# Reordering the preparation of a seven-product step in the FFN's down projection, and the last output scaling

## The chip, the cores and the metric

The kernel runs on one core of a Trainium2 chip. The metric is device time in microseconds; the kernel before took 1753.55 us (median of 3 runs, 1753.36 to 1753.64). The engines are named as the profile names them: PE (TensorE matmul), PEld (its weight loads), DVE (VectorE), ACT (ScalarE), POOL (GpSimd), SP (the queue that issues most DMAs).

## What is computed

One decoder layer on 256 tokens of width 2048, in float32: a normalisation, one combined projection, dilated-window attention beside a gated recurrence, an output projection with a residual, and a feed-forward part. The change lies in the last of these lines, the down projection (5632 to 2048 columns) and the norm and residual behind it:

```python
a = rmsnorm(h, norm_ffn_pre[layer])
gt, up = jnp.split(a @ w_ffn_gate_up[layer], [D_FF], axis=-1)
ff = (jax.nn.silu(gt) * up) @ w_ffn_down[layer]
h = h + rmsnorm(ff, norm_ffn_post[layer])
```

## The kernel before

**Precision.** Every float32 operand is split in two parts: a high part (fp32r, made by a copy on ACT) and a low part (the operand minus its high part, made by a subtraction on DVE). A product of two operands is three matmuls: high x high, high x low, low x high.

**Steps of the down projection.** The output has 2048 columns, taken in two blocks of 1024 (two groups of 512). Each block runs over 22 steps; a step takes 256 rows of the weights (a tile `raw` of 128 x 2048) and the matching two chunks of the activation (`act`, 2 x 128 x 256). The 256 tokens are two sides of 128.

- An **ordinary step** makes 2 sides x 2 groups x 2 chunks = 8 products, so 24 matmuls.
- A **seven-product step** makes the same 2 x 2 x 2 block product from 7 products of sums and differences of sub-blocks (a Strassen-Winograd scheme), so 21 matmuls, and pays for it with sums of the weights and sums of the activation. There are six of them in each block, every third step (`DOWN`): steps 4, 7, ..., 19 of the first block and 3, 6, ..., 18 of the second. The first of its products uses `dh` and `dl`, the high and low parts of three of the four raw weight sub-blocks; `dl` is the last tile that is prepared.

**Preparation of a step** (`split_wide`) first calls `prep_act`, which splits the activation (`a`: high on ACT L410, low on DVE L411). For a seven-product step it also makes four sums `s` of the activation on DVE (L379, L379, L382, L383, in `seven_sums`), their high part `so` on ACT (L384) and low part on DVE (L385). After that it treats the weights. For an ordinary step this is the high part `w` (ACT L305) and the low part `wl` (DVE L306). For a seven-product step it is three DVE instructions for the sums `sum` (L310, L316, L317), their high parts `w` on ACT (L315, L318), `dh` on ACT (L320), and the low parts `wl` (L321) and `dl` (L322) on DVE.

**What sets the order.** The schedule is manual: each engine runs its instructions in the order in which the program writes them, and waits for another engine or a DMA at the head of its queue. The main loop writes, for each step i: the preparation of step i+2, the load of step i+5 (SP, L289, two DMAs of 512 KB), the matmuls of step i, and evacuation work of an earlier block. The buffers bound how far an engine can run ahead: 3 of `raw`, 3 of `w`, 3 of `wl`, 1 each of `sum`, `dh`, `dl`. So the high part of step i+2 needs the `w` buffer that PE frees when it has finished step i-1, and the load of step i+5 needs the `raw` buffer that ACT and DVE free when they have prepared step i+2.

**The end.** The last three steps are run side by side, and `finish(i, j)` handles side i and column group j = 2, 3. It adds the partial result (L1191, `down_sum`), squares it on ACT with a running sum (L1195, `down_square`), and for j = 2 multiplies by the gain (`down_gain`, L1200). For j = 3 it computes the norm factor `r3` (`rsqrt_mean`: DVE L127, L129, L133 and ACT L125, L126), then writes four stores, each a DVE instruction (L1241: result times `r3` plus residual) and a DMA. The gain multiplication of group 3 stands ahead of the last store.

Of the kernel before, what the change touches and what calls it, by code (L numbers as in the profile page):

```python
# [13 lines left out]
F32 = mybir.dt.float32  # L14
F32R = mybir.dt.float32r
I32 = mybir.dt.int32
AF = mybir.ActivationFunctionType
# [60 lines left out]
def tile_hybrid_block(ctx: ExitStack, tc: tile.TileContext, t, out):  # L78
    nc = tc.nc
# [12 lines left out]
    def nm(s):  # L92
        serial[0] += 1
        return f"{s}_{serial[0]}"

    def rslot(s):
        return rpool.tile([P, 1024], F32R, tag="r", bufs=16, name=nm(s))
# [10 lines left out]
    def p3(s, dtype, n, bufs, tag=None):  # L108
        return act_pool[0].tile([P, n], dtype, tag=tag or s, bufs=bufs, name=nm(s))
# [7 lines left out]
    def rsqrt_mean(dst, ss, n, bias=None):  # L117

        w = ss.shape[-1]
        v, y, a = (small(s)[:, :w] for s in ("v", "y", "a"))
        bias = bias or (eps[:, 0:1], eps[:, 1:2])
        nc.scalar.activation(y, ss, AF.Ln, scale=1.0 / n, bias=bias[0])  # L125
        nc.scalar.activation(y, y, AF.Exp, scale=-0.5)  # L126
        nc.vector.tensor_scalar(v, ss, -0.5 / n, bias[1], op0=OP.mult, op1=OP.add)  # L127
        if w == 1:
            nc.vector.scalar_tensor_tensor(out=a, in0=y, scalar=v, in1=y, op0=OP.mult, op1=OP.mult)  # L129
        else:  # L130
            nc.vector.tensor_mul(a, y, y)
            nc.vector.tensor_mul(a, a, v)
        nc.vector.scalar_tensor_tensor(  # L133
            out=dst, in0=a, scalar=1.5, in1=y, op0=OP.add, op1=OP.mult
        )
# [31 lines left out]
    def ptile(s):  # L167
        pool, n = (act_pool[0], 2) if act_pool else (fp, 5)
        return pool.tile([P, 512], F32, tag="p", bufs=n, name=nm(s))
# [58 lines left out]
    def wslot():  # L228
        return stream.tile([P, 2048], F32R, tag="w", bufs=N_SPLIT, name=nm("w"))
# [65 lines left out]
    def split_wide(n):  # L295

        if n >= len(steps):
            return
        b, i, raw = steps[n][:3]
        m, by7 = b.order[i]  # L300
        if b.prep:
            b.prep(m, by7)
        hi, lo = wslot(), p3("wl", F32R, 2048, 3)
        if not by7:
            nc.scalar.activation(hi, raw, AF.Copy)  # L305
            nc.vector.tensor_sub(lo, raw, hi.bitcast(F32))  # L306
            steps[n][3] = hi, lo
            return
        s, d = p3("sum", F32, 2048, 1), raw[:, 512:]
        nc.vector.tensor_sub(  # L310
            s[:, :1024].rearrange("p (a c) -> p a c", a=2),
            raw[:, 512:1536].rearrange("p (a c) -> p a c", a=2),
            raw[:, None, :512].to_broadcast([P, 2, 512]),
        )
        nc.scalar.activation(hi[:, :1024], s[:, :1024], AF.Copy)  # L315
        nc.vector.tensor_add(s[:, 1024:1536], raw[:, 512:1024], s[:, 512:1024])  # L316
        nc.vector.tensor_sub(s[:, 1536:], raw[:, 1536:], s[:, 1024:1536])  # L317
        nc.scalar.activation(hi[:, 1024:], s[:, 1024:], AF.Copy)  # L318
        dhi, dlo = p3("dh", F32R, 1536, 1), p3("dl", F32R, 1536, 1)
        nc.scalar.activation(dhi, d, AF.Copy)  # L320
        nc.vector.tensor_sub(lo, s, hi.bitcast(F32))  # L321
        nc.vector.tensor_sub(dlo, d, dhi.bitcast(F32))  # L322
        steps[n][3] = hi, lo, dhi, dlo

# [49 lines left out]
    def seven_sums(f, dst):  # L374

        s = ptile("s").rearrange("p (n t) -> p n t", n=4)
        a11, a12, a21, a22 = f[:, 0, :P], f[:, 1, :P], f[:, 0, P:], f[:, 1, P:]
        for o, x, c, y in ((0, a21, -1.0, a22), (1, s[:, 0, :], -1.0, a11)):
            nc.vector.scalar_tensor_tensor(  # L379
                out=s[:, o, :], in0=x, scalar=c, in1=y, op0=OP.mult, op1=OP.subtract  # L380
            )
        nc.vector.tensor_sub(s[:, 2, :], a11, a21)  # L382
        nc.vector.tensor_sub(s[:, 3, :], a12, s[:, 1, :])  # L383
        nc.scalar.activation(dst[:, 0], s, AF.Copy)  # L384
        nc.vector.tensor_sub(dst[:, 1], s, dst[:, 0].bitcast(F32))  # L385

    def sums_of(dst):
        return lambda n: (dst[:, 0, n, :], dst[:, 1, n, :])


    class Split:
# [14 lines left out]

        def put(self, n, src):

            x = self.slots[n]
            nc.scalar.activation(x[:, :, 0, :], src, AF.Copy)  # L410
            nc.vector.tensor_sub(x[:, :, 1, :], src, x[:, :, 0, :].bitcast(F32))  # L411
            self.there.add(n)

# [677 lines left out]
    def h_sums():  # L1091

        for m in H7:
            f = ptile("f").rearrange("p (k t) -> p k t", k=2)
            x = hT[0].slots[m]
            nc.vector.tensor_add(f, x[:, :, 0, :].bitcast(F32), x[:, :, 1, :].bitcast(F32))
            dst = p3("so", F32R, 1024, 4).rearrange("p (z n t) -> p z n t", z=2, n=4)
            yield
            seven_sums(f, dst)
            h7[m] = sums_of(dst)  # L1100
            yield

# [71 lines left out]
            )  # L1174

    def prep_act(m, by7):
        f = act_t[m // 2][:, m % 2 * 2 : m % 2 * 2 + 2, :]
        x = parts_of[m] = Split("a", 2)
        x.put(0, f)
        if by7:  # L1180
            dst = rslot("so").rearrange("p (z n t) -> p z n t", z=2, n=4)
            seven_sums(f, dst)
            a7[m] = sums_of(dst)

    def act(k):
        return parts_of[k // 2](k % 2)

    def down_sum(j, i, b):

        f = b.rest[i, j % 2]  # L1190
        nc.vector.tensor_add(f, b.bank[i, j % 2], f)  # L1191

    def down_square(j, i, b):
        sq, r2 = fss[0][:, 4 * i + j : 4 * i + j + 1], r2c[:, i : i + 1]
        nc.scalar.activation(ptile("junk"), b.rest[i, j % 2], AF.Square, scale=r2, accum_out=sq)  # L1195

    def down_gain(j, i, b):
        if i == 0:
            fz[j] = p3("fz", F32, 1024, 4, "so").rearrange("p (b c) -> p b c", b=2)
        nc.vector.scalar_tensor_tensor(  # L1200
            out=fz[j][:, i, :], in0=b.rest[i, j % 2], scalar=r2c[:, i : i + 1],
            in1=fpost[j // 2][:, (j % 2) * 512 : (j % 2 + 1) * 512],
            op0=OP.mult, op1=OP.mult,
        )
# [11 lines left out]
    def so_far_of(ss, i):  # L1216

        b = small("base")
        nc.vector.tensor_reduce(
            b[:, 0:1], ss[:, 4 * i : 4 * i + 3], op=OP.add, axis=mybir.AxisListType.X  # L1220
        )
        nc.vector.tensor_scalar(b[:, 0:1], b[:, 0:1], 1.0 / D, EPS, op0=OP.mult, op1=OP.add)
        nc.vector.tensor_scalar(b[:, 1:2], b[:, 0:1], -0.5, None, op0=OP.mult)
        return b[:, 0:1], b[:, 1:2]
# [3 lines left out]
    def finish(i, j):  # L1228

        b = wides[-1]  # L1230
        down_sum(j, i, b)
        down_square(j, i, b)
        if j == 2:
            down_gain(j, i, b)
            bases[i] = so_far_of(fss[0], i)
            return
        sq, r3 = fss[0][:, 4 * i + 3 : 4 * i + 4], r3c[:, i : i + 1]

        def store(j, lo=0, hi=512, eng=nc.sync):
            z = fz[j][:, i, lo:hi]  # L1240
            nc.vector.scalar_tensor_tensor(  # L1241
                out=z, in0=z, scalar=r3, in1=h_t[j][:, i, lo:hi], op0=OP.mult, op1=OP.add
            )
            eng.dma_start(out[0, i * P : (i + 1) * P, j * 512 + lo : j * 512 + hi], z)

        rsqrt_mean(r3, sq, D, bases[i])
        store(0, 0, 128)
        store(0, 128, 512, nc.scalar)
        store(1)
        store(2, eng=nc.scalar)  # L1250
        down_gain(3, i, b)
        store(3)


# [52 lines left out]
    for j in range(2):  # L1307
        add_wide_block(t["w_ffn_down"][0], (1024 * j, 1024 * j + 512), DOWN[j], act,
                       lambda m: a7[m], evac_down, prep=prep_act,
                       pre=begin_down if j == 0 else None, turn=3 if j == 0 else None)  # L1310
# [14 lines left out]
    for i in range(len(chunks)):  # L1325
        b, c = chunks[i][:2]
# [17 lines left out]
    for i in range(len(steps)):  # L1344
        b, c = steps[i][:2]
# [22 lines left out]
    for g in range(2):  # L1368
        multiply_wide(last, (0,), (g,))
        finish(0, 2 + g)  # L1370
    for g in range(2):
        for i in (last - 2, last - 1, last):
            multiply_wide(i, (1,), (g,))
        finish(1, 2 + g)
# [51 lines left out]
```

## Time and profile before

| | |
|---|---|
| median of the runs | 1753.55 us |
| the profiled execution's own time | 1753.68 us |
| its span | 1751.9 us |
| DVE busy over the span | 1265.1 us (72%) |
| ACT busy over the span | 885.0 us (51%) |
| first matmul of the down projection | starts at 1500.83 us |
| last matmul of the program | starts at 1741.25 us |
| last DVE instruction | starts at 1747.80 us, lasts 0.75 us |

How to read it: times are from the start of the span. The down projection is the last seventh of it, and only this stage is touched by the change. Matmuls are pipelined: a row of PE lasts 0.39 us while the next starts 0.23 us later, so PE's busy share says little, and stalls of PE are read from the distance between starts. DVE's rows overlap a little too: a 128x2048 subtraction lasts 2.28 us and the next instruction starts 2.20 us after it.

### The profile page before, as it was taken

How to read it: one execution, taken by the hardware profiler on the slowest of the kernel's cores; microseconds unless marked ns; L12 is line 12 of the kernel's file. 1: busy time of each engine (PE TensorE's matmuls, PEld its weight loads, DVE VectorE, ACT ScalarE, POOL GpSimd, SP SyncE). 2: the span in 40 equal slices, each digit the busy share in tenths (PEclk: the TensorE clock that was granted, in tenths of full speed). 3: DMA queues.
4: the chain of work that ended last, by engine and by line, in shares of the span. 5: the costliest groups of instructions: out<-in, count | busy, mean ns of one | idle time of the engine just before them, and what ended most of it. 6: DMA issues, size and time to landing. Idle time of an engine off the chain costs nothing.

```text
span 1751.9 us, 21592 instructions
## 1 busy us (share of the span) xinstructions
PE 1730.3 (99%) x8424; PEld 1449.0 (83%) x8424; DVE 1265.1 (72%) x1372; ACT 885.0 (51%) x1050; POOL 74.1 (4%) x54
## 2 busy tenths in 40 slices
PE   9999999999999999999999999999999999999997
PEld 7888888888888888888888877888888888878775
DVE  5657657877546775544565577888888888888887
ACT  6545445344444444454444465555555555565563
POOL 0002404300000000000000000000000000000000
PEclk9999999999999999999999999999999999999999
DMA  7655444455455554455555745555555555656553
GB/s 265 204 191 193 144 162 151 145 165 182 159 169 169 189 188 161 159 175 193 194 183 189 268 157 203 194 192 193 204 206 204 201 194 192 223 181 218 183 183 117
DMA packets 201223, 325.92 MB, mean 186 GB/s; under 512 B 10096, under 2 KB 76832, under 8 KB 201120
## 3 DMA queue, kind: packets, MB, share of 16 engines
q1 hardware_dynamic: 198848, 319.41, 54.2%
q10 hardware_dynamic: 2272, 5.12, 0.8%
q8 instruction: 66, 1.08, 0.2%
q14 instruction: 37, 0.30, 0.1%
HBM read 322.40 MB, written 2.10 MB: 185 GB/s over the span
## 4 chain that ended last, share of the span: by engine, by line
PE 82%; DVE 12%; ACT 3%; issue 2%; DMA 1%; POOL 0%; SPq 0%; DVEq 0%; ACTq 0%
PE acc L115 65%; PE aux L115 16%; DVE wl L306 3%; DVE wl L321 1%; DVE dl L322 1%; DVE a L411 1%; DVE sum L310 1%; ACT w L318 1%; DVE w L243 1%; DVE sum L317 0%; DVE sum L316 0%; ACT w L242 0%; DVE w L667 0%; ACT so L384 0%; DVE s L379 0%
## 5 line engine op out<-in xcount | busy, mean ns | idle before, releaser
L243 DVE TENSOR_TENSOR w<-raw,w 128x1024 fp32r<-128x1024 f32 (+1 forms) x353 | 444.2, 1260 | 366.4 <-ACT w L242 364.3
L242 ACT ACTIVATE w<-raw 128x1024 fp32r<-128x1024 f32 (+1 forms) x353 | 373.0, 1057 | 483.1 <-PE acc L115 472.1
L115 PE MATMUL acc<-w,xT 128*128 128x512 f32 x1728 | 407.9, 394 | 0.0
L115 PEld LDWEIGHTS acc<-w,xT 128*128 128x128 f32 x1728 | 325.1, 190 | 65.7 <-DVE w L243 0.3
L115 PE MATMUL acc<-xT,w 128*128 128x512 f32 (+1 forms) x2048 | 365.5, 340 | 0.0
L115 PEld LDWEIGHTS acc<-xT,w 128*128 128x128 f32 x2048 | 314.8, 189 | 46.1
L306 DVE TENSOR_TENSOR wl<-raw,w 128x2048 fp32r<-128x2048 f32 x82 | 187.4, 2285 | 19.9 <-ACT w L305 19.9
L305 ACT ACTIVATE w<-raw 128x2048 fp32r<-128x2048 f32 x82 | 156.4, 1908 | 59.0 <-PE aux L115 27.0
L115 PE MATMUL acc<-w,hT 128*128 128x512 f32 x622 | 182.5, 392 | 1.5 <-DVE w L243 1.2
L115 PEld LDWEIGHTS acc<-w,hT 128*128 128x128 f32 x622 | 115.8, 188 | 27.0 <-DVE w L243 2.5
L115 PE MATMUL aux<-w,hT 128*128 128x512 f32 x430 | 135.6, 389 | 0.0
L321 DVE TENSOR_TENSOR wl<-sum,w 128x2048 fp32r<-128x2048 f32 x42 | 96.3, 2292 | 47.3 <-ACT w L318 47.3
L115 PEld LDWEIGHTS aux<-w,hT 128*128 128x128 f32 x430 | 80.7, 188 | 16.8
L315 ACT ACTIVATE w<-sum 128x1024 fp32r<-128x1024 f32 x42 | 44.6, 1063 | 96.3 <-DVE sum L310 92.0
L115 PE MATMUL acc<-w,yT 128*128 128x512 f32 x384 | 88.0, 390 | 0.2 <-DVE w L243 0.2
L115 PEld LDWEIGHTS acc<-w,yT 128*128 128x128 f32 x384 | 71.9, 188 | 15.4 <-DVE w L243 0.6
L115 PE MATMUL acc<-w,a 128*128 128x512 f32 x268 | 83.7, 389 | 0.0
L115 PE MATMUL aux<-w,a 128*128 128x512 f32 x268 | 83.7, 389 | 0.0
L115 PE MATMUL aux<-wl,hT 128*128 128x512 f32 x215 | 83.6, 389 | 0.0
L115 PE MATMUL acc<-wl,hT 128*128 128x512 f32 x215 | 83.6, 389 | 0.0
L322 DVE TENSOR_TENSOR dl<-raw,dh 128x1536 fp32r<-128x1536 f32 x42 | 73.5, 1751 | 0.0
L320 ACT ACTIVATE dh<-raw 128x1536 fp32r<-128x1536 f32 x42 | 61.9, 1473 | 0.0
(263 smaller groups left out, 2016.9 us busy)
## 6 DMA issues: line engine op xcount, KB each, us to landing
raw<-in_w_in SPq DMA_DIRECT2D x271, 512.0 KB, 4.5
raw<-in_w_ffn_gate_up SPq DMA_DIRECT2D x176, 512.0 KB, 4.4
raw<-in_w_ffn_down SPq DMA_DIRECT2D x88, 512.0 KB, 4.9
raw<-in_w_mix_out SPq DMA_DIRECT2D x32, 512.0 KB, 4.9
raw<-in_w_attn_branch SPq DMA_DIRECT2D x16, 512.0 KB, 4.6
raw<-in_w_hgrn_branch SPq DMA_DIRECT2D x16, 512.0 KB, 4.6
hx<-in_x ACTq DMA_DIRECT2D x4, 512.0 KB, 9.9
x<-in_x SPq DMA_DIRECT2D x3, 512.0 KB, 10.4
```

The lines of the kernel that those rows point to most:

```text
L115: nc.tensor.matmul(ps, lhsT, rhs, start=start, stop=stop, skip_group_check=True)
L242: nc.scalar.activation(wh[:, k], raw[:, k], AF.Copy)
L243: nc.vector.tensor_sub(wl[:, k], raw[:, k], wh[:, k].bitcast(F32))
L305: nc.scalar.activation(hi, raw, AF.Copy)
L306: nc.vector.tensor_sub(lo, raw, hi.bitcast(F32))
L310: nc.vector.tensor_sub(s[:, :1024].rearrange("p (a c) -> p a c", a=2), raw[:, 512:1536].rearrange("p (a c) -> p a c", a=2), raw[:, None, : ...
L315: nc.scalar.activation(hi[:, :1024], s[:, :1024], AF.Copy)
L318: nc.scalar.activation(hi[:, 1024:], s[:, 1024:], AF.Copy)
L320: nc.scalar.activation(dhi, d, AF.Copy)
L321: nc.vector.tensor_sub(lo, s, hi.bitcast(F32))
L322: nc.vector.tensor_sub(dlo, d, dhi.bitcast(F32))
L411: nc.vector.tensor_sub(x[:, :, 1, :], src, x[:, :, 0, :].bitcast(F32))
```

## The change

The generator `prep_act` is cut into pieces, and `split_wide` calls the pieces at chosen places. An ordinary step keeps its order. In a seven-product step the activation's high part still comes first; then the sums of the weights and their high parts; then the activation's low part and its four sums with their high part; then `dh` and `wl`; then the low part `so` of the activation's sums; and `dl` last. In the gate-up blocks no activation is prepared, so nothing moves there. In `finish`, the gain multiplication of group 3 moves up, to directly behind the square that ACT computes.

```diff
         b, i, raw = steps[n][:3]
         m, by7 = b.order[i]
-        if b.prep:
-            b.prep(m, by7)
+        prep = b.prep(m, by7) if b.prep else iter(())
+        next(prep, None)
         hi, lo = wslot(), p3("wl", F32R, 2048, 3)
         if not by7:
             nc.scalar.activation(hi, raw, AF.Copy)
+            next(prep, None)
             nc.vector.tensor_sub(lo, raw, hi.bitcast(F32))
...
         nc.scalar.activation(hi[:, 1024:], s[:, 1024:], AF.Copy)
+        next(prep, None)
         dhi, dlo = p3("dh", F32R, 1536, 1), p3("dl", F32R, 1536, 1)
         nc.scalar.activation(dhi, d, AF.Copy)
         nc.vector.tensor_sub(lo, s, hi.bitcast(F32))
+        next(prep, None)
         nc.vector.tensor_sub(dlo, d, dhi.bitcast(F32))
...
         nc.scalar.activation(dst[:, 0], s, AF.Copy)
-        nc.vector.tensor_sub(dst[:, 1], s, dst[:, 0].bitcast(F32))
+        return lambda: nc.vector.tensor_sub(dst[:, 1], s, dst[:, 0].bitcast(F32))
...
-            seven_sums(f, dst)
+            seven_sums(f, dst)()
...
         x = parts_of[m] = Split("a", 2)
-        x.put(0, f)
+        x.high(0, f)
+        yield
+        x.low(0, f)
         if by7:
             dst = rslot("so").rearrange("p (z n t) -> p z n t", z=2, n=4)
-            seven_sums(f, dst)
+            low = seven_sums(f, dst)
             a7[m] = sums_of(dst)
+            yield
+            low()
...
         down_square(j, i, b)
+        down_gain(j, i, b)
         if j == 2:
-            down_gain(j, i, b)
             bases[i] = so_far_of(fss[0], i)
             return
...
         store(2, eng=nc.scalar)
-        down_gain(3, i, b)
         store(3)
```

**DVE, the first seven-product step of the down projection.** The names are those of the section on the kernel; `act` is the activation, `a` its parts. Before:

```order
L411 TENSOR_TENSOR a_11413<-act_8972,a_11413 128x2x256
L379 SCALAR_TENSOR_TENSOR s_11417<-act_8972 128x128
L379 SCALAR_TENSOR_TENSOR s_11417<-s_11417,act_8972 128x128
L382 TENSOR_TENSOR s_11417<-act_8972 128x128
L383 TENSOR_TENSOR s_11417<-act_8972,s_11417 128x128
L385 TENSOR_TENSOR so_11416<-s_11417,so_11416 128x512
L310 TENSOR_TENSOR sum_11426<-raw_11300 128x1024
L316 TENSOR_TENSOR sum_11426<-raw_11300,sum_11426 128x512
L317 TENSOR_TENSOR sum_11426<-raw_11300,sum_11426 128x512
L321 TENSOR_TENSOR wl_11425<-sum_11426,w_11424 128x2048
L322 TENSOR_TENSOR dl_11433<-raw_11300,dh_11432 128x1536
```

The same step on DVE in the changed kernel:

```order
L311 TENSOR_TENSOR sum_11417<-raw_11300 128x1024
L317 TENSOR_TENSOR sum_11417<-raw_11300,sum_11417 128x512
L318 TENSOR_TENSOR sum_11417<-raw_11300,sum_11417 128x512
L420 TENSOR_TENSOR a_11413<-act_8972,a_11413 128x2x256
L382 SCALAR_TENSOR_TENSOR s_11425<-act_8972 128x128
L382 SCALAR_TENSOR_TENSOR s_11425<-s_11425,act_8972 128x128
L385 TENSOR_TENSOR s_11425<-act_8972 128x128
L386 TENSOR_TENSOR s_11425<-act_8972,s_11425 128x128
L323 TENSOR_TENSOR wl_11416<-sum_11417,w_11415 128x2048
L388 TENSOR_TENSOR so_11424<-s_11425,so_11424 128x512
L325 TENSOR_TENSOR dl_11432<-raw_11300,dh_11431 128x1536
```

The three sums of the weights moved to the front, and the low part `so` moved from behind the activation's sums to between `wl` and `dl`.

**ACT, the same step.** Before:

```order
L410 ACTIVATE a_11413<-act_8972 128x2x256
L384 ACTIVATE so_11416<-s_11417 128x512
L315 ACTIVATE w_11424<-sum_11426 128x1024
L318 ACTIVATE w_11424<-sum_11426 128x1024
L320 ACTIVATE dh_11432<-raw_11300 128x1536
```

And in the changed kernel:

```order
L416 ACTIVATE a_11413<-act_8972 128x2x256
L316 ACTIVATE w_11415<-sum_11417 128x1024
L319 ACTIVATE w_11415<-sum_11417 128x1024
L387 ACTIVATE so_11424<-s_11425 128x512
L322 ACTIVATE dh_11431<-raw_11300 128x1536
```

On ACT only the high part `so` moved, from ahead of the two high parts of the weights' sums to behind them.

**DVE, the end of the program (side 1, group 3).** Here `e` is the partial result, `fss` the sums of squares from ACT, `fz` the output tiles, `h` the residual. Before:

```order
L1191 TENSOR_TENSOR e_12954<-acc_12238,e_12954 128x512
L127 TENSOR_SCALAR v_13084<-fss_11334,base_13059 128x1
L129 SCALAR_TENSOR_TENSOR a_13086<-y_13085,v_13084 128x1
L133 SCALAR_TENSOR_TENSOR r3c<-a_13086,y_13085 128x1
L1241 SCALAR_TENSOR_TENSOR fz_12247<-fz_12247,r3c,h_7825 128x128
L1241 SCALAR_TENSOR_TENSOR fz_12247<-fz_12247,r3c,h_7825 128x384
L1241 SCALAR_TENSOR_TENSOR fz_12302<-fz_12302,r3c,h_7860 128x512
L1241 SCALAR_TENSOR_TENSOR fz_13002<-fz_13002,r3c,h_7903 128x512
L1200 SCALAR_TENSOR_TENSOR fz_13033<-e_12954,r2c,fpost_11337 128x512
L1241 SCALAR_TENSOR_TENSOR fz_13033<-fz_13033,r3c,h_7967 128x512
```

In the changed kernel:

```order
L1205 TENSOR_TENSOR e_12954<-acc_12238,e_12954 128x512
L1214 SCALAR_TENSOR_TENSOR fz_13017<-e_12954,r2c,fpost_11337 128x512
L127 TENSOR_SCALAR v_13085<-fss_11334,base_13059 128x1
L129 SCALAR_TENSOR_TENSOR a_13087<-y_13086,v_13085 128x1
L133 SCALAR_TENSOR_TENSOR r3c<-a_13087,y_13086 128x1
L1255 SCALAR_TENSOR_TENSOR fz_12247<-fz_12247,r3c,h_7825 128x128
L1255 SCALAR_TENSOR_TENSOR fz_12247<-fz_12247,r3c,h_7825 128x384
L1255 SCALAR_TENSOR_TENSOR fz_12302<-fz_12302,r3c,h_7860 128x512
L1255 SCALAR_TENSOR_TENSOR fz_13002<-fz_13002,r3c,h_7903 128x512
L1255 SCALAR_TENSOR_TENSOR fz_13017<-fz_13017,r3c,h_7967 128x512
```

The gain multiplication (L1200, now L1214) moved from ahead of the last store to directly behind the sum, ahead of the small instructions of the norm. PE's instructions and the DMAs keep their order.

More of the change, by code (lines that the diff above doesn't have):

```diff
@@ L407, in put, with high, low @@
         def put(self, n, src):
+            self.high(n, src)
+            self.low(n, src)
+        def high(self, n, src):
+            nc.scalar.activation(self.slots[n][:, :, 0, :], src, AF.Copy)
+        def low(self, n, src):
             x = self.slots[n]
-            nc.scalar.activation(x[:, :, 0, :], src, AF.Copy)
             nc.vector.tensor_sub(x[:, :, 1, :], src, x[:, :, 0, :].bitcast(F32))
```

## The prediction

> **What bounds the kernel now.** I read the page first, then the waits of the last 270 us (the down projection and the end), then the timelines of DVE, ACT and PE there. The page's first line makes PE look like the only bound:
>
> ```profile
> PE 1730.3 (99%) x8424; PEld 1449.0 (83%) x8424; DVE 1265.1 (72%) x1372; ACT 885.0 (51%) x1050; POOL 74.1 (4%) x54
> ```
>
> That is an average over stages. In the window from 1480 us on, the waits (total, times, longest) say otherwise:
>
> ```profile
> DVE wl L321 <- ACT w L318: 14.6, 13, 1.1
> ...
> DVE so L385 <- ACT so L384: 8.4, 12, 0.7
> ...
> PE acc L115 <- DVE dl L322: 2.7, 5, 1.6
> ...
> PE aux L115 <- DVE dl L322: 1.6, 6, 0.3
> ```
>
> PE waits for DVE's `dl` in 11 of the 12 seven-product steps, and DVE itself stands idle twice in each of these steps, for ACT. One period (a seven-product step and the two ordinary ones behind it) on DVE's timeline:
>
> ```profile
> 1513.37 0.68 DVE L411 TENSOR_TENSOR a<-act,a 128x512 fp32r<-128x512 f32 x1
> ...
> 1515.69 0.69 DVE L385 TENSOR_TENSOR so<-s,so 128x512 fp32r<-128x512 f32 x1 [0.70 <-ACT so L384]
> 1516.30 1.22 DVE L310 TENSOR_TENSOR sum<-raw 128x1024 f32<-128x1024 f32 x1
> ...
> 1518.28 0.69 DVE L317 TENSOR_TENSOR sum<-raw,sum 128x512 f32<-128x512 f32 x1
> 1520.10 2.29 DVE L321 TENSOR_TENSOR wl<-sum,w 128x2048 fp32r<-128x2048 f32 x1 [1.13 <-ACT w L318]
> 1522.31 1.75 DVE L322 TENSOR_TENSOR dl<-raw,dh 128x1536 fp32r<-128x1536 f32 x1
> 1523.97 0.68 DVE L411 TENSOR_TENSOR a<-act,a 128x512 fp32r<-128x512 f32 x1
> ...
> 1529.58 0.69 DVE L411 TENSOR_TENSOR a<-act,a 128x512 fp32r<-128x512 f32 x1
> ```
>
> The period is 1529.58 - 1513.37 = 16.21 us: 10.60 us for the seven-product step (with 0.70 + 1.13 us of idling) and 5.61 us for two ordinary steps. What PE would need without waits comes from an undisturbed stretch of the chain that ended last:
>
> ```profile
> 1484.67 7.48 PE acc L115 x33
> ```
>
> 7.48 / 33 = 0.2267 us per matmul. A period has 24 + 24 + 21 = 69 matmuls, so 15.64 us. DVE's 16.21 us is longer, so **in the down projection DVE sets the pace**, through its two idle gaps, and PE loses about 0.55 us in each period. PE's starts show the loss. `dh`, `dl`, `dh` are three matmuls in a row, so the first and third should start 0.45 us apart (2 x 0.2267):
>
> ```profile
> 1523.39 0.48 PE L115 MATMUL aux<-dh,a 128*128 128x512 f32 x1
> ...
> 1524.45 0.40 PE L115 MATMUL aux<-dh,a 128*128 128x512 f32 x1
> ...
> 1652.66 0.39 PE L115 MATMUL acc<-dh,a 128*128 128x512 f32 x1
> 1654.66 0.50 PE L115 MATMUL acc<-dl,a 128*128 128x512 f32 x1 [1.61 <-DVE dl L322]
> 1654.99 0.39 PE L115 MATMUL acc<-dh,a 128*128 128x512 f32 x1
> ...
> 1718.87 0.39 PE L115 MATMUL acc<-dh,a 128*128 128x512 f32 x1
> ...
> 1719.83 0.40 PE L115 MATMUL acc<-dh,a 128*128 128x512 f32 x1
> ```
>
> The first of the eleven loses 1.06 - 0.45 = 0.61 us, the last 0.96 - 0.45 = 0.51; with the eight of the same kind between them, read from their starts, ten stalls make 5.44 us. The eleventh, at 1654.66 us, loses 2.33 - 0.45 = 1.88 us: before it DVE had evacuated the first block. A twelfth stall, in the last step, is for `wl`:
>
> ```profile
> 1729.41 0.61 PE L115 MATMUL acc<-w,a 128*128 128x512 f32 x2
> 1730.68 0.50 PE L115 MATMUL acc<-wl,a 128*128 128x512 f32 x1 [0.66 <-DVE wl L306]
> 1731.02 0.62 PE L115 MATMUL acc<-w,a 128*128 128x512 f32 x2
> ```
>
> The second matmul of the row at 1729.41 starts at 1729.64, so 1.38 us stand where 0.45 would do: 0.93 us. **PE's loss to DVE is 5.44 + 1.88 + 0.93 = 8.25 us.**
>
> **The change, part one: the seven-product step.** No engine's work changes, only order, in 12 steps. *The wait for `so` (0.70 us)*: DVE now runs the 2.2 us of `wl` between the activation's sums and the low part `so`. *The wait for `w` (1.13 us)*: between the last weights' sum and `wl` DVE now does the activation's low part and four sums, which take 1515.69 - 0.70 - 1513.37 = 1.62 us in the rows above, longer than the gap. Whether ACT keeps up follows from its own rows of the same step:
>
> ```profile
> 1515.02 0.63 ACT L384 ACTIVATE so<-s 128x512 fp32r<-128x512 f32 x1 [5.18 <-DVE s L383]
> ...
> 1519.00 1.06 ACT L318 ACTIVATE w<-sum 128x1024 fp32r<-128x1024 f32 x1 [0.31 <-DVE sum L317]
> 1519.97 1.47 ACT L320 ACTIVATE dh<-raw 128x1536 fp32r<-128x1536 f32 x1
> ```
>
> Count from the start of DVE's first weights' sum. The third ends at 1518.28 + 0.69 - 1516.30 = 2.67 us; ACT's second high part then ends near 3.8; DVE ends the activation's sums near 4.3, so `wl` starts with no wait. ACT makes `so` (to 5.0) and `dh` (to 6.4); DVE ends `wl` near 6.5, does the low part `so` to 7.1, then `dl`, for which `dh` is there. The step takes 10.60 - 1.83 = 8.77 us, a period 16.21 - 1.83 = 14.38 us. That is 1.26 us less than PE's 15.64. So DVE gains on PE until it is held by the three `w` buffers: PE frees the buffer of a seven-product step 48 matmuls, 10.88 us, before that step's first matmul. Even if DVE began the whole 8.77 us only then, `dl` would be in time. Hence none of the eleven stalls should be left, and 30% of the removed idling (0.57 of 1.83) is enough for the ordinary ones. The stall of 1.88 us lies behind two seven-product steps, in which DVE gains up to 3.66 us. The last `wl` waits for ACT, and ACT for the load:
>
> ```profile
> 1717.68 1.75 DVE L322 TENSOR_TENSOR dl<-raw,dh 128x1536 fp32r<-128x1536 f32 x1
> ...
> 1724.87 1.92 ACT L305 ACTIVATE w<-raw 128x2048 fp32r<-128x2048 f32 x1 [2.09 <-DMA raw<-in_w_ffn_down]
> ```
>
> From `dl`'s end (1719.43), which frees `raw`, to ACT's start are 5.44 us; with `dl` earlier against PE this load is in time. I take all **8.25 us**. Bounds: the rows marked as waits before PE sum to 2.7 + 1.6 + 0.66 = 4.96 us, and from PE's first matmul of the stage to its last about 8.6 us are lost.
>
> **Part two: the end.** The chain runs over DVE:
>
> ```profile
> 1732.14 0.69 DVE L1191 TENSOR_TENSOR e<-acc,e 128x512 f32<-128x512 f32 x1 [1.51 <-PE acc L115]
> ...
> 1740.31 0.68 DVE L1191 TENSOR_TENSOR e<-acc,e 128x512 f32<-128x512 f32 x1
> ...
> 1742.33 0.68 DVE L1191 TENSOR_TENSOR e<-acc,e 128x512 f32<-128x512 f32 x1
> 1743.89 0.21 DVE L127 TENSOR_SCALAR v<-fss,base 128x1 f32<-128x1 f32 x1 [0.88 <-ACT junk L1195]
> ...
> 1747.02 0.75 DVE L1200 SCALAR_TENSOR_TENSOR fz<-e,r2c,fpost 128x512 f32<-128x512 f32 x1
> 1747.80 0.75 DVE L1241 SCALAR_TENSOR_TENSOR fz<-fz,r3c,h 128x512 f32<-128x512 f32 x1
> ```
>
> The multiplication costs 1747.80 - 1747.02 = 0.78 us and moves into a gap of 0.88 us in which DVE waits for ACT's square. For side 1 that is 0.75 us off the end. Side 0 has the same shape, and side 1's first sum (1740.31) follows it directly on DVE, so 0.7 us more, unless side 1's last sum then waits for PE. PE's last matmul is modelled to end at 1741.64, 9.50 us behind the start at 1732.14; without the multiplication DVE gets there after 1742.33 - 1732.14 - 0.72 = 9.47 us. It just fits: together about 1.43 us. What can eat into this is the transfer of the last four stores, 1.05 MB, which DVE would then emit within 2.95 us:
>
> ```profile
> 1747.00:1748.00 1.00, 0.00 (x0) 0.00 (x0) 0.96 (x3) 0.00 (x0) 0.00 (x0) 0.50 0.89 325
> ```
>
> At the 325 GB/s of this row, 1.05 MB take 3.2 us, so up to 0.2 us may be lost; I take **1.3 us**, with bounds 0.7 (one side only) and 1.5. The Trainium skill (DMA: Bandwidth & Descriptors, section Anatomy of one DMA — SWDGE (gpsimd) path) gives a transfer that GpSimd issues as about 2.0 us plus its bytes over 436 GB/s. By that figure 1.05 MB would move in an estimated 2.4 us, nothing would be lost, and the sum would be 0.13 us larger; the row shows a lower rate.
>
> **The sum**: 1753.68 - 8.25 - 1.3 = **1744.1 us**, against the profiled execution's own time; the median of the runs lies 0.13 us lower.
>
> **Rivals.**
>
> *Only part of the idling goes.* If `wl` still waits for ACT, 0.70 us of each step are saved: the period is 15.51 us, still under PE's 15.64. The ordinary stalls go (5.44), of the big one 2 x 0.70 = 1.4, the last one stays: 1753.68 - 5.44 - 1.4 - 1.3 = 1745.5 us. For it speaks that ACT's high parts now stand in front of `so`; against it the 1.62 us of cover over a gap of 1.13.
>
> *DVE is not what PE waits for.* If DVE only passes on the lateness of the loads, its gaps reopen elsewhere and the end alone is gained: 1753.68 - 1.3 = 1752.4 us. Against it: the weights' sum at 1516.30 starts without a wait, so its load was there.
>
> *Slower: the load at the head of DVE's queue.* Before, a seven-product step began with work on the activation, which needs no load. Now its first instruction reads `raw`, and behind it stands all of DVE. That buffer is freed by the seven-product step before, and DVE comes back after two ordinary steps, 5.61 us later; the load took 5.44 us. Each us beyond 5.61 is idling in every period. At 5.61 + 1.83 = 7.4 us the gain is gone. At 8.0 us the period would be 14.38 + 2.39 = 16.77 us, 0.56 above today's, so 11 x 0.56 - 1.3 = 4.9 us slower: 1758.6 us. Against it: the longest landing among the stage's loads is 6.7 us,
>
> ```profile
> DMA to landing us min/median/max: 3.7/4.8/6.7
> ```
>
> and once PE sets the pace the buffer is freed 15.64 - 8.77 = 6.9 us or more before DVE needs it.
>
> **How the numbers follow.** All of it as forecast, 1743 to 1746 us: 0.80. Part of the idling, or loads late by a fraction, 1745 to 1749: 0.12. Only the end: 0.05. The late load, slower: 0.03. The lower end is the sum with its best bounds, 1753.68 - 8.6 - 1.5 = 1743.6, less the 0.13 to the median and the scatter: 1743.0. The upper end takes the worst bounds, 1753.68 - 4.96 - 0.7 = 1748.0, and a little of the second case: 1748.5. A measurement of this kernel can tell about 0.2% (3.5 us) from no change. Beyond that, faster: the first case and nearly all of the second, 0.92. Within it: 0.05. Slower: 0.03.
>
> **What would show it.** In the profile of the changed kernel PE's waits for `dl` should be gone; a period should be near 15.64 us; DVE's waits for `so` and for the weights' high part should be gone in the down projection, and ACT should wait for PE instead, for a free `w` buffer. The last matmul should start near 1741.25 - 8.25 = 1733.0 us and the last DVE instruction near 1738.1. The prediction is wrong if the weights' first sum shows waits for a DMA, if `wl` still waits for ACT, or if PE's matmuls start further apart than 0.2267 us without any wait.

## The result and the profile after

| | before | after |
|---|---|---|
| median of the runs, first comparison (6 and 6 runs) | 1753.60 us | 1742.39 us |
| ratio, 95% interval | | 0.9934 [0.9921, 0.9947] |
| median, a later comparison (9 and 5 runs) | 1752.78 us | 1742.99 us |
| ratio, 95% interval | | 0.9947 [0.9934, 0.9961] |
| the profiled execution's own time / its span | 1753.68 / 1751.9 us | 1742.44 / 1740.6 us |
| first matmul of the down projection starts at | 1500.83 us | 1499.22 us |
| first to last matmul of the down projection (starts) | 240.42 us | 231.87 us |
| last matmul's start to the end of the last DVE instruction | 7.31 us | 5.88 us |
| from there to the end of the span | 3.30 us | 3.64 us |

The change makes the kernel faster by some 10 us. The forecast was 1744.1 us with a range from 1743.0; the first comparison gave 1742.39 us, below the range. Of all the runs compared here and below, one stood apart and is left out of its ratio: a run of e3 (the experiments below) that took 2146.44 us at a mean granted clock of 0.751. The table splits the 11.25 us by which the two spans differ: 8.55 us in the down projection, 1.43 at the end on DVE, -0.34 given back behind the last DVE instruction, and **1.61 us ahead of the stage, in code that the change does not touch**.

The chain that ended last, by engine, in the kernel before:

```profile
PE 82%; DVE 12%; ACT 3%; issue 2%; DMA 1%; POOL 0%; SPq 0%; DVEq 0%; ACTq 0%
```

and in the changed one:

```profile
PE 95%; DVE 2%; ACT 1%; DMA 1%; issue 1%; POOL 0%; SPq 0%; DVEq 0%; ACTq 0%
```

It is now PE almost throughout. The waits of the changed kernel from 1500 us on (engine, line, waited for: us in total, times, longest):

```profile
ACT w L316 <- DVE sum L311: 38.4, 12, 4.9
ACT w L305 <- issue: 22.3, 10, 2.4
DVE wl L307 <- ACT w L305: 15.9, 14, 1.7
...
ACT w L305 <- PE aux L115: 7.6, 3, 3.0
ACT so L387 <- DVE s L386: 5.7, 12, 0.5
```

No row of PE is left in this view, and none of DVE waiting for `so` or for the high part of the weights' sums. DVE now idles in the ordinary steps, for ACT's high part, and ACT in turn for PE or for nothing that the profile shows; that this is the free `w` buffer is inferred. One period on DVE's timeline, far into the first block:

```profile
1557.57 1.22 DVE L311 TENSOR_TENSOR sum<-raw 128x1024 f32<-128x1024 f32 x1
...
1559.54 0.69 DVE L318 TENSOR_TENSOR sum<-raw,sum 128x512 f32<-128x512 f32 x1
1560.15 0.69 DVE L420 TENSOR_TENSOR a<-act,a 128x512 fp32r<-128x512 f32 x1
...
1561.69 2.29 DVE L323 TENSOR_TENSOR wl<-sum,w 128x2048 fp32r<-128x2048 f32 x1
1563.89 0.68 DVE L388 TENSOR_TENSOR so<-s,so 128x512 fp32r<-128x512 f32 x1
1564.49 1.75 DVE L325 TENSOR_TENSOR dl<-raw,dh 128x1536 fp32r<-128x1536 f32 x1
...
1570.99 2.29 DVE L307 TENSOR_TENSOR wl<-raw,w 128x2048 fp32r<-128x2048 f32 x1 [1.35 <-ACT w L305]
1573.20 1.22 DVE L311 TENSOR_TENSOR sum<-raw 128x1024 f32<-128x1024 f32 x1
```

The seven-product step runs from 1557.57 to 1566.16 us, 8.6 us, without a gap inside; the period is 15.63 us, PE's. And PE at a seven-product step:

```profile
1537.52 0.39 PE L115 MATMUL aux<-dh,a 128*128 128x512 f32 x1
1537.74 0.39 PE L115 MATMUL aux<-dl,a 128*128 128x512 f32 x1
1537.97 0.39 PE L115 MATMUL aux<-dh,a 128*128 128x512 f32 x1
```

The first and third start 0.45 us apart; the same step of the kernel before had 1.00 us there (1539.66 to 1540.66). The end on DVE (side 1):

```profile
1729.44 0.68 DVE L1205 TENSOR_TENSOR e<-acc,e 128x512 f32<-128x512 f32 x1
...
1731.52 0.69 DVE L1205 TENSOR_TENSOR e<-acc,e 128x512 f32<-128x512 f32 x1
1732.24 0.75 DVE L1214 SCALAR_TENSOR_TENSOR fz<-e,r2c,fpost 128x512 f32<-128x512 f32 x1
1733.09 0.21 DVE L127 TENSOR_SCALAR v<-fss,base 128x1 f32<-128x1 f32 x1
...
1734.10 2.87 DVE L1255 SCALAR_TENSOR_TENSOR fz<-fz,r3c,h 128x128 f32<-128x128 f32 x5
```

The multiplication at 1732.24 fills the time in which ACT squares; L127 starts 1.57 us behind the start of the sum, 1.56 before. The four stores' five DVE instructions now run as one piece of 2.87 us, and their data goes out at once:

```profile
1736.00:1737.00 1.00, 0.00 (x0) 0.00 (x0) 0.97 (x2) 0.00 (x0) 0.00 (x0) 0.50 0.91 329
1737.00:1738.00 1.00, 0.00 (x0) 0.00 (x0) 0.00 (x0) 0.00 (x0) 0.00 (x0) 0.50 1.08 375
```

The last columns of these windows are the DMA engines' busy share (a packet's whole time counts where it starts) and GB/s; the 0.50 before them is PE's granted clock, with no work left for PE. The last store landed 2.72 us after its issue, against 2.38 before, and this is the 0.34 us given back; that the crowding of the stores makes it is argued.

What is left are the 1.61 us ahead of the stage. The windows between 332 and 340 us show where they come from, in the kernel before:

```profile
332.00:336.00 4.00, 4.00 (x22) 3.51 (x22) 3.86 (x5) 0.00 (x0) 0.00 (x0) 0.72 0.69 236
336.00:340.00 4.00, 4.00 (x22) 3.48 (x21) 1.57 (x2) 2.10 (x3) 0.30 (x1) 0.85 0.02 7
```

and in the changed one:

```profile
332.00:336.00 4.00, 4.00 (x26) 3.61 (x27) 3.86 (x5) 0.32 (x1) 0.00 (x0) 1.00 0.63 217
336.00:340.00 4.00, 4.00 (x25) 3.48 (x25) 1.79 (x3) 3.33 (x6) 2.14 (x3) 1.00 0.21 56
```

The third number from the right is the granted clock of PE. In the profiled execution of before it was at half for 3.41 us from 333.8 us on (and once more, in both kernels, near 307 us); this second stretch, worth an estimated 3.41 / 2 = 1.7 us where PE sets the pace, is missing in the changed kernel's profile.

### The profile page after: what moved, and what is told of

The parts are those of the page before. It is cut to its first block, busy times and chain, and to the rows that moved or that the text cites. A ratio compares the mean times of both kernels' runs of the same rounds, so it can differ in the third digit from the quotient of the medians.

```text
span 1740.6 us, 21588 instructions
## 1 busy us (share of the span) xinstructions
PE 1725.5 (99%) x8424; PEld 1448.5 (83%) x8424; DVE 1264.6 (73%) x1372; ACT 886.2 (51%) x1050; POOL 74.1 (4%) x54
## 4 chain that ended last, share of the span: by engine, by line
PE 95%; DVE 2%; ACT 1%; DMA 1%; issue 1%; POOL 0%; SPq 0%; DVEq 0%; ACTq 0%
PE acc L115 71%; PE aux L115 22%; DVE w L243 1%; ACT w L242 0%; DVE w L676 0%; PE aux L723 0%; PE aux L452 0%; DMA gpost<-in_norm_mix_post 0%; DMA x<-in_x 0%; PE acc L1126 0%; DVE fz L1255 0%; PE aux L1126 0%; DVE x L775 0%; PE aux L439 0%; ACT junk L1209 0%
```

## The experiments

Three theories stood against each other. A: PE is freed of its waits for DVE and the end is shortened, some 9.6 us, and what changed ahead of the stage is not the change's. B: the change is worth all of the 11.2 us. E, on the cause of the rest: the stretches of half clock come by chance, behind little work on PE.

All profiles in one table: the stage's begin and length, the stretch behind the last matmul up to DVE's end, the number of early stretches of half clock (some at 211 us, some at 307, some at 333; one at 211 us lasted 6.83 us and counts as two), and the span.

| kernel | stage begins | stage lasts | behind it | half clock | span |
|---|---|---|---|---|---|
| before | 1500.83 | 240.42 | 7.31 | 2 | 1751.9 |
| after | 1499.22 | 231.87 | 5.88 | 1 | 1740.6 |
| e1 split only | 1501.64 | 231.87 | 7.38 | 3 | 1744.2 |
| e2 tail only | 1501.89 | 240.49 | 5.88 | 3 | 1751.9 |
| e3 `so` last | 1499.82 | 232.33 | 5.88 | 2 | 1741.7 |
| e4 sums first | 1499.51 | 231.87 | 5.88 | 2 | 1740.9 |
| e5 dose 1 | 1502.56 | 233.81 | 5.98 | 3 | 1746.0 |
| e6 dose 2 | 1501.70 | 247.32 | 5.88 | 3 | 1758.5 |
| e7 before, spare matmuls | 1497.91 | 240.43 | 7.32 | 0 | 1749.0 |
| e8 after, spare matmuls | 1497.59 | 231.87 | 5.88 | 0 | 1738.9 |
| e9 after again | 1499.78 | 231.87 | 5.88 | 2 | 1741.2 |
| e10 after, at the idle time | 1496.88 | 231.87 | 5.88 | 0 | 1738.3 |
| e11 after, at the narrow matmuls | 1497.48 | 231.87 | 5.88 | 0 | 1738.9 |

### The two parts of the change alone

**e1**, the changed kernel with the old end:

```diff
         down_square(j, i, b)
-        down_gain(j, i, b)
         if j == 2:
+            down_gain(j, i, b)
...
         store(2, eng=nc.scalar)
+        down_gain(3, i, b)
         store(3)
```

> The step's new order alone, with the end as it was before. Theory A (PE is freed of its waits for DVE in the down projection, and nothing else moves): first to last matmul of the stage 231.9 us as in the changed kernel (240.4 before), the stretch from the last matmul's start to the last DVE instruction's end 7.3 us as before, so about 1753.6 - 8.5 = 1745.1 us, or 1743.4 if the trace shows one stretch of half granted clock fewer in the early, untouched part. Rival B (the 1.6 us that the changed kernel gained ahead of the stage belong to the change): 1743.5 us, and the stage begins 1.6 us earlier than before in every run.

Measured: 1745.18 us, ratio 0.995 [0.9933, 0.9966]. Against the kernel before in the same comparison (1752.45 us) that is 7.3 us, less than the 8.55 of the stage; the stretches of half clock, which vary from run to run as shown further down, blur medians of so few runs, so the parts are read from the profiles. The stage has its 231.87 us, the end is as before: ahead of L127, DVE waits again.

```profile
1736.22 0.21 DVE L127 TENSOR_SCALAR v<-fss,base 128x1 f32<-128x1 f32 x1 [0.88 <-ACT junk L1209]
```

**e2**, the kernel before with the new end only (the same lines, the other way round):

> Only the gain multiplication moves, the step keeps its old order. Theory A: the stage from first to last matmul stays at 240.4 us, the stretch behind the last matmul shrinks by 1.4 us, of which 0.3 are given back by the transfers of the last stores: about 1752.5 us (1750.8 with one stretch of half clock fewer early). Rival B: 1752.5 us and the stage begins where it did before.

Measured: 1752.01 us, ratio 0.9996 [0.9987, 1.0006], which cannot be told from no change in the time (1.1 us were forecast, 0.4 came out); the profile shows the change, with 5.88 us behind the last matmul in place of 7.31, while the stage's 240.49 us and the old waits stand:

```profile
DVE so L385 <- ACT so L384: 8.4, 12, 0.7
```

In both kernels the stage begins later than in the kernel before (1501.64 and 1501.89 us, with three early stretches of half clock each, where the kernel before had two), not 1.6 us earlier. Since e1 holds the whole new order of the step, B has little left.

### Half of the new order

**e3** puts the activation's work ahead of the weights' sums again and only the low part of its sums behind `wl`:

```diff
         x.high(0, f)
-        yield
         x.low(0, f)
         if by7:
...
             a7[m] = sums_of(dst)
             yield
+            yield
             low()
```

> The changed kernel, but the activation's parts and sums stand ahead of the weights' sums as before; only their low part is put behind the weights' low part. DVE loses only the wait of 0.70 us for the activation's sums and keeps the 1.13 us. Theory A: DVE's period is 16.21 - 0.70 = 15.51 us, still under PE's 15.64, so nearly all of PE's stalls go: 232 to 233 us from first to last matmul, 1742.4 to 1744 us. Rival C (the gain is in proportion to the idling removed, 0.70 of 1.83): 240.4 - 3.3 = 237.1 us, about 1747.7 us.

**e4** keeps the weights' sums first, but does the low part of the activation's sums at once:

```diff
             a7[m] = sums_of(dst)
-            yield
             low()
```

> The changed kernel, but the low part of the activation's sums follows directly behind the sums, so DVE waits there for ACT and only the wait of 1.13 us goes. Theory A: period 16.21 - 1.13 = 15.08 us, under PE's 15.64: first to last matmul 231.9 us, 1742.4 us as the changed kernel. Rival C (in proportion, 1.13 of 1.83): 240.4 - 5.3 = 235.1 us, about 1745.6 us.

Measured: e3 1744.68 us (three runs), 0.9946 [0.993, 0.9963] of the time before, stage 232.33 us; e4 1742.98 us, 0.994 [0.9925, 0.9955], stage 231.87 us. The stage of e3 is where A has it, its time is 0.7 us above A's range. Removing 0.70 of the 1.83 us brings 8.09 of the 8.55 us, removing 1.13 us brings all. C falls: the gain is capped by PE's 15.64 us, and either half of the new order reaches the cap, or all but 0.46 us of it.

### More work for DVE

**e5** and **e6** compute the first weights' sum of each seven-product step two and three times (the result is the same):

```diff
-        nc.vector.tensor_sub(
+        for _ in range(2 if b.prep else 1):
+            nc.vector.tensor_sub(
...
```

> The changed kernel with the first weights' sum of each of the 12 seven-product steps of the down projection computed twice: 1.25 us more on DVE per period. Theory A: DVE's period rises from 14.38 to 15.63 us, just PE's 15.64, so the slack is used up and almost nothing is lost: first to last matmul of the stage 231.9 to 233.0 us. Rival D (DVE stays the pace-setter, the old waits were not what mattered): 11 x 1.25 = 13.8 us more, 245.6 us.

> The same sum computed three times: 2.50 us more on DVE per period. Theory A: period 16.88 us, 1.24 us over PE's 15.64; PE waits for DVE again in about eleven steps, 1.24 us each, a little more at the first step and behind the evacuation of the first block: 231.9 + 15 = 247 us (245 to 249) from first to last matmul, about 1757 us. Rival D: 11 x 2.50 = 27.5 us more, 259.4 us.

Measured: e5 1745.06 us and a stage of 233.81 us, 1.94 more than the changed kernel's: far from D's 13.8, but 0.8 above A's own range. PE's waits for DVE in the stage of e5:

```profile
PE acc L115 <- DVE dl L326: 0.5, 1, 0.5
PE acc L115 <- DVE wl L307: 0.3, 1, 0.3
```

The single `dl` stands at 1683 us, in the second block. Ten us before it, DVE waited for a load:

```profile
1673.63 2.48 DVE L312 TENSOR_TENSOR sum<-raw 128x1024 f32<-128x1024 f32 x2 [1.11 <-DMA raw<-in_w_ffn_down]
```

This is the late load of the prediction's slower case. Without these 1.11 us `dl` would have been ready in time; PE lost 0.67 us there. In the same way e4 has two such waits (0.9 us together, with no wait of PE behind them) and e6 one of 0.6. The `wl` stands in the last step, where evacuation work (four sums from 1720.07 to 1722.94 us) loads DVE too. At a period equal to PE's there is no slack for either. e6: 1758.82 us and 247.32 us, inside A's 245 to 249. On DVE the sums of two steps in a row start 16.74 us apart (the view ends inside the second group, so its last sum is missing), and PE waits again:

```profile
1530.97 3.75 DVE L312 TENSOR_TENSOR sum<-raw 128x1024 f32<-128x1024 f32 x3
...
1547.71 2.48 DVE L312 TENSOR_TENSOR sum<-raw 128x1024 f32<-128x1024 f32 x2
```

```profile
1541.09 0.39 PE L115 MATMUL aux<-dh,a 128*128 128x512 f32 x1
1542.23 0.50 PE L115 MATMUL aux<-dl,a 128*128 128x512 f32 x1 [0.76 <-DVE dl L326]
1542.57 0.39 PE L115 MATMUL aux<-dh,a 128*128 128x512 f32 x1
```

This step loses 1.48 - 0.45 = 1.03 us. Part of the 247.32 us is a stretch of half clock that came inside the stage, at 1659.1 us, as PE's longest stall (1657.25 to 1659.67 us) ended.

### The part ahead of the stage

Where do the stretches of half clock come? In the kernel before, PE's timeline shows an idle time ahead of the one at 307 us, and ahead of the one at 333 us narrow matmuls, which keep PE busy with 64 columns and then with one:

```profile
305.10 2.41 PE L115 MATMUL aux<-x 128*128 128x64 f32 x16 [1.41 <-DVE x L766]
...
329.39 1.89 PE L115 MATMUL aux<-x 128*128 128x64 f32 x16
331.12 1.90 PE L115 MATMUL aux<-ones,x 128*128 128x1 f32 x16
```

**e7** (the kernel before) and **e8** (the changed kernel) put spare matmuls on zeros there:

```diff
             ps = aux()
+            for _ in range(6 if half == 1 and lev == 2 else 0):
+                mm(ps, warm[:, :P], warm, True, True)
             for e in range(8):
                 xe = x[:, e * P : (e + 1) * P]
...
             ps = aux()
+            for _ in range(3):
+                mm(ps, warm[:, :P], warm, True, True)
             for e in range(8):
                 mm(ps[:, e : e + 1], x[:, e * P : (e + 1) * P], ones[:, 0:1], True, True)
```

> The kernel before, with spare matmuls on zeros in the early, untouched part: six ahead of the level of the second recurrence in whose place PE idles for 1.7 us, and three ahead of the sixteen matmuls of one column in each of the two recurrences. Theory E (what moved ahead of the stage is the number of 3.41 us stretches of half granted clock, which come at 211, 307 and 333 us behind little work on PE): no such stretch left, the stage begins at 1498.5 to 1499.5 us in the profile instead of 1500.8, and the runs lie closer together; about 1751.5 us. Rival F (the stretches are not caused by that idling): the stretches remain, and the spare matmuls cost 1.3 us: 1754 us.

> The changed kernel with the same spare matmuls. Theory E: no stretch of half clock in the early part, the stage begins where it does in the kernel before with spare matmuls, and the difference between the two is what the stage and the end give, 8.55 + 1.1 = 9.6 us: about 1742 us. Rival B (the change itself is worth 11.2 us): 11.2 us between the two.

Measured: e7 1751.14 us (11 runs), e8 1741.22 us (5 runs, 1740.76 to 1741.37). No stretch is left in either profile; a window of e8:

```profile
332.00:336.00 4.00, 4.00 (x25) 3.55 (x24) 2.64 (x4) 1.72 (x3) 0.00 (x0) 1.00 0.28 97
```

The stage begins at 1497.91 and 1497.59 us, 0.3 us apart and no longer 1.6, and **the two medians differ by 9.92 us**, the spans by 10.01. B's 11.2 falls; E stands as far as that spare work on PE at these places takes the stretches away in the profiles. Two points do not fit as well: the stage of e7 begins 0.6 us earlier than E's range, and of e7's runs (1750.52 to 1752.98 us) nine have a mean granted clock of 0.998 but the two slowest 0.997, so a stretch may have been left in these.

The table allows one more test. Less 1.7 us for each early stretch, the stage begins at 1497.4 us in the kernel before and at 1497.5 in the changed one, so in this pair nothing of the 1.61 us is left to the change. Over all 13 profiles this figure lies between 1496.1 and 1497.9 us; what makes that remainder is not shown, and a few tenths of a us either way cannot be told.

The median of e8 is also the lowest of all, 0.993 [0.9917, 0.9944] of the time before.

**e9, e10, e11** ask which place matters, beside the changed kernel again (e10 has the first of the two edits, e11 the second):

> The changed kernel once more, beside the two that follow, for how often the early stretches of half clock come. Theory E: between none and three of them in a profile, so the stage begins anywhere from 1497.6 to 1502 us, and the runs scatter by 2 us or more around 1742 to 1744 us, while first to last matmul of the stage stays at 231.9 us. Rival B: 1742.4 us with the stage beginning at 1499.2 us.

> The changed kernel with only the six spare matmuls in PE's idle time of 1.7 us. Theory E: the stretch at 307 us goes, those at 211 and 333 us, which come behind the matmuls of one column, still come in some runs; the six matmuls cost nothing, since PE idled there. About 1742 us, with the scatter that the other two stretches leave.

> The changed kernel with only the spare matmuls ahead of the matmuls of one column (2 x 3, some 1.3 us of PE time). Theory E: the stretches at 211 and 333 us go, the one at 307 us, behind the idle 1.7 us, comes in nearly every run: the stage begins near 1497.6 + 1.5 = 1499.1 us, about 1742.8 us with little scatter.

Measured: e9 1742.99 us (1741.72 to 1745.05), as E expects; its profile has stretches at 212.7 and 332.1 us and none at 307, although PE idled there. e10 1741.70 us (1740.07 to 1743.10), as E expects. e11 (median 1744.36 us) missed: its runs fall into two groups, 1740.68 and 1740.88 beside 1744.36 to 1744.49 us, and the profiled one, of the lower group, has no stretch at 307 us either, although PE idled there. The 3.5 us between the groups would be two stretches, and the mean granted clocks fit (0.998 and 0.999 below, 0.996 to 0.997 above), but no profile shows the upper group. So the two places together keep the stretches away in what was profiled, and what each of them does alone stays open.

## Why the prediction came out as it did

**What bounds the kernel: right.** DVE set the pace of the down projection. Freed by 0.70, 1.13 or 1.83 us per step, it stops doing so (e3, e4, after); given 2.50 us, it does so again (e6).

**Part one, 8.25 us: right, 8.55 measured.** The three kinds of stall are all gone, the one behind the first block's evacuation and the last `wl` included. The 0.3 us more are within the upper bound given there (8.6), the whole loss between the stage's first and last matmul.

**Part two, 1.3 us: right in the mechanism, 1.09 measured.** DVE ends 1.43 us earlier against PE, as worked out. The transfers of the last stores gave back 0.34 us where 0.2 was the worst and 0.13 was taken. The row of 325 GB/s allowed a little more than was read from it: 1.05 MB take 3.23 us at that rate, 0.28 over the 2.95. By the Trainium skill's figure for transfers that GpSimd issues (DMA: Bandwidth & Descriptors, Anatomy of one DMA — SWDGE (gpsimd) path) nothing would have been lost; here SP and ACT issue the stores, and the trace shows the loss of 0.34 us.

**The rivals.** Partial removal of the idling was priced at 1745.5 us with a stage gain of 5.44 + 1.4 us; e3, which is that case, gained 8.09: the last stall went as well. The loads were not late: the weights' first sum, which now heads DVE's queue, shows no wait for a DMA, so the slower case did not come up in the changed kernel. It is not far off: e4, e5 and e6 each show such waits, up to 1.11 us.

**The step that failed** is the sum's footing: "1753.68 - 8.25 - 1.3", made against one profiled execution as if all ahead of the stage stood still (its variation was put at nothing), and with it the lower end, "1753.68 - 8.6 - 1.5 = 1743.6, less the 0.13 to the median and the scatter: 1743.0". The terms add up to 9.64 us measured against 9.55 forecast; the other 1.61 us lie ahead of the stage and are not the change's (e7 and e8). The scatter was taken from three runs that lay within 0.28 us. In the later comparisons the same kernel ran from 1749.92 to 1754.88 us, with medians of 1752.45, 1752.78 and 1753.08, all below the 1753.68 that the sum starts from. Between none and three stretches of half clock, 1.7 us each, would account for this spread, and the mean granted clocks on record go with it: 0.998 for the fastest run, 0.995 to 0.996 for those above 1754 us. They could be seen in the profile of before: the granted clock's windows of 0.72 to 0.85 near 307 and 333 us were there to be read, and a range that allowed one stretch more or fewer would have begun at 1743.0 - 1.7 = 1741.3 us. The first comparison's 11.2 us held some of this luck; 9.8 us (e9's comparison) and 9.92 us (e7 against e8) are the better figures for the change.

## What to carry to other kernels

Where two engines take turns in a stage, compare the period of each, idle gaps included; the engine with the longer one sets the pace, and filling its gaps with independent work of its own queue pays until the other one's period is reached, and nothing beyond it (0.70 of 1.83 us were nearly enough here). Before a sum is made against one profile, look at the granted clock over the whole span and at the distance between landmarks ahead of the change: what differs there from run to run belongs in the range. And where a change moves a landmark that it cannot reach, test the two kernels with that cause taken away before the gain is believed.

## What the runs showed of the hardware

- PE's granted clock fell to half for 3.41 us at a time, in a kernel on one core in which PE is busy 99% of the span. It came behind an idle time of PE of 1.7 us (start to start), at the end of a stall of PE of 2.4 us, start to start (e6), and also where PE did not idle at all but ran narrow matmuls for about 3.5 us; not in every execution (e9 and e11 have the idle time and no stretch behind it). Within one execution the stretches start whole multiples of 3.413 us apart (333.77 - 306.47 = 27.30 us, 8 of them, in the kernel before), and where this grid lies against the program differs between executions; that this decides whether a stretch comes is argued. The Trainium skill (TensorE: Matmul & The Clock Gate, What's actually happening) has a free-running window of about 3.4 us and half the clock after at least one idle window. The length of the stretches and the grid agree; that an idle time of half a window, or a window of busy but narrow matmuls, can be enough is more than that section says.
- Spare matmuls cost nothing where PE idled: from the last wide matmul before the idle time to the first narrow one behind it are 1.70 us without them (e9) and 1.70 us with them (e10). With those at both places no profile has an early stretch, and the runs of e8 lie within 0.6 us, those of the changed kernel within 3.3 us (e9); those of the kernel before with them (e7) still spread over 2.5 us.
- Four output stores of 1.05 MB in all, put out by DVE within 2.9 us, ran at up to 375 GB/s (in a window of 1 us), and the last of them landed 0.34 us later against DVE than when they were spread over 3.7 us.
